# A transformer block in fp32 on one core: the second sums of weights added by a transfer from DRAM instead of by VectorE

## The chip, the core and the metric

The kernel runs on one core of a Trainium2 chip. The metric is the device time of one execution in microseconds (us), from launch to the last output byte. Engines are named as in the profile: PE is TensorE (matmuls), PEld its weight loads, DVE is VectorE, ACT is ScalarE, POOL is GpSimd, SP is SyncE. Sixteen DMA engines serve all transfers of the core. Transfers come to them from queues: q1 holds those that SP issues, q0 those that POOL issues, q10 those that ACT issues.

## What is computed

One block on 256 tokens of width 2048, all in fp32: a half-step SwiGLU feed-forward layer (2048 to 5632 and back), a mixing stage (one wide projection, attention over chunks, retention, gates, output projections), a second feed-forward layer like the first, and a last norm.

```python
def swiglu_ffn(x, w_gate, w_up, w_down):
    return (jax.nn.silu(x @ w_gate) * (x @ w_up)) @ w_down

x = x + 0.5 * swiglu_ffn(rmsnorm(x, norm_ffn1_g), ffn1_w_gate, ffn1_w_up, ffn1_w_down)
h = rmsnorm(x, norm_mix_g)
proj = h @ w_in            # q, k, v of attention; q, k, v, g of retention; two gates
...
merged = sigmoid(gate_a) * (att @ w_out_att) + sigmoid(gate_r) * (ret @ w_out_ret)
x = x + merged @ w_out
x = x + 0.5 * swiglu_ffn(rmsnorm(x, norm_ffn2_g), ffn2_w_gate, ffn2_w_up, ffn2_w_down)
return rmsnorm(x, norm_final_g)
```

## The kernel before

**Precision.** PE multiplies in a shorter format, so every weight tile is split into a high part and the rest (`split`, L138 to L142): ACT casts the tile to its high part (L140), DVE subtracts that from the tile to get the low part (L141), and each product takes three matmuls (L151, L152, L154). A tile of weights is 128 x 2 x 512 floats, 512 KB.

**Two kinds of steps.** The program is a list of steps (entries), about 1,080 in all. A standard step (`standard`) loads one tile into a ring of five raw buffers, splits it and multiplies it for both halves of the tokens, 12 matmuls. The other steps belong to groups of a Strassen-Winograd scheme (`Strassen`): two blocks of 512 output columns over the whole depth of 2048 are computed with seven products instead of eight. There are 26 groups: ten in each feed-forward layer and six in the mixing stage. A group takes 28 steps of 6 matmuls, in four phases, each over four pieces `jc` of the depth. Standard steps are woven between them (`weave`).

**The weights of a group.** For each `jc`, a group loads the upper half's tile of the first matrix (`k`) and of the second (`x`), on POOL's queue, into eight to ten kept buffers that are shared with the next group (`loads`, L540). In a feed-forward layer the first matrix is w_up and the second w_gate; in the mixing stage both are parts of w_in. Then sums are made in place:

- the first sum, x = x + k: by DVE (L529), or for one or two of the four pieces by a transfer with an add, from SBUF to SBUF (`add_on`, L545);
- the second sum, x = x + the lower tile of the second matrix: by DVE (L597), when that tile, loaded by SP into a raw buffer, is split for its own product in phase 1;
- the third, in `third`: k = x - k by DVE (L583), and x = x + the lower tile of the first matrix by a transfer with an add, straight from DRAM (L584).

A group's step is split as `r` (of a tile as it was loaded) or `s` (of a sum). In the profile a tile `hiz22610s` is the high part in group z226, phase 1, piece 0, of a sum. In phase 0 the `s` steps split the first sum, in phase 1 the second, in phase 2 k, in phase 3 the third.

**What sets the order.** Each engine works off its own list in program order and waits on semaphores. `run` goes through the steps: at step c it first prepares (splits) steps up to c + 4, then calls whatever was set for step c by `later(n, fn)`, which means n steps after the step at hand, then issues the products of step c. `load_some` issues a load as soon as a buffer of its ring is free. POOL's list therefore holds, in one order, the loads of k and x, the transfers with an add, and a few small operations; a transfer that waits holds up all behind it.

Of the kernel before, what the change touches and what calls it, by code (L numbers as in the profile page):

```python
# [11 lines left out]
ALU = mybir.AluOpType  # L12
# [33 lines left out]
FIRST_ADDED = (2, 3)  # L46
MIX_AHEAD = 12
FIRST_WAIT = 4
LAST_SUM = 24
ROTATED = {("q", 0): (6, 7), ("k", 0): (5, 6), ("q", 1): (4, 5), ("k", 1): (3, 4)}  # L50
HEAD_AT = (3, 6, 10, 13, 17, 20, 24, 27)
# [4 lines left out]
ADD_WAIT = 6  # L56
# [30 lines left out]
def block_kernel(ctx: ExitStack, tc: tile.TileContext, x, g1, w1g, w1u, w1d, gm, w_in, rel, woa, wor, wo,  # L87
                 g2, w2g, w2u, w2d, gf, cos, sin, decay, ident, out):
    nc = tc.nc
# [30 lines left out]
    def later(n, fn):  # L120
        due.setdefault(state["step"] + n, []).append(fn)

    def weights_tile(name):
        return wpool.tile([P, KC, NB], F32, tag="raw", bufs=RAW_BUFS, name=name)

    def chunk(w, r0, c0):
        return w[r0 : r0 + KC * P, c0 : c0 + NB].rearrange("(k p) n -> p k n", p=P)

    def fetch(t, w, r0, c0, parts=(slice(0, KC),)):
        for p in parts:  # L130
            nc.sync.dma_start(t[:, p, :], chunk(w, r0, c0)[:, p, :])

    def split_tiles(name):
        return [
            wpool.tile([P, KC, NB], F32R, tag=tag, bufs=SPLIT_BUFS, name=f"{tag}{name}") for tag in ("hi", "lo")
        ]

    def split(raw, name):  # L138
        hi, lo = split_tiles(name)
        nc.scalar.copy(hi, raw)  # L140
        nc.vector.tensor_sub(lo, raw, hi.bitcast(F32))  # L141
        return hi, lo  # L142
# [3 lines left out]
    def three(products, read_between=False):  # L146


        more = {"skip_group_check": True} if read_between else {}
        for acc, (ahi, alo), (whi, _), first, _ in products:  # L150
            nc.tensor.matmul(acc, ahi, whi, start=first, stop=False, **more)  # L151
            nc.tensor.matmul(acc, alo, whi, start=False, stop=False, **more)  # L152
        for acc, (ahi, _), (_, wlo), _, last in products:
            nc.tensor.matmul(acc, ahi, wlo, start=False, stop=last, **more)  # L154
# [216 lines left out]
    class Operand:  # L371


        def __init__(self, name, n):
            self.hi, self.lo, self.name = [None] * n, [None] * n, name
# [18 lines left out]
    class Norm:  # L394
# [40 lines left out]
        def put(self, b, halves=(0, 1), between=None):  # L435
# [28 lines left out]
            elif 1 in halves and b % 2 == 1:  # L464
                for i, key in enumerate(self.SUMS):
                    wait = LAST_SUM if key == "s7" and self.name != "n1" and b == D // NB - 1 else 1 + 3 * i
                    later(wait, lambda key=key: self.add_up(b // 2, key))
# [39 lines left out]
    class Strassen:  # L507
# [3 lines left out]

        def __init__(self, norm, w1, col1, w2, col2, evict, added=()):
            self.added, self.summed = added, set()
            self.add_wait, self.early = ADD_WAIT, False
            self.norm, self.w, self.col, self.evict = norm, (w1, w2), (col1, col2), evict
            self.x, self.kept, self.acc, self.wide = {}, {}, {}, {}
            self.name = f"z{len(steps)}"
# [17 lines left out]
        def loads(self):  # L535
# [11 lines left out]
            def second(jc):  # L547
# [3 lines left out]
                elif self.early:  # L551
                    later(FIRST_WAIT, lambda: self.first_once(jc))

# [16 lines left out]
        def step(self, phase, jc, of_sum):  # L570
            made = {}
            name = f"{self.name}{phase}{jc}{'rs'[of_sum]}"
            n = HALF_K // KC

            def load():
                made["raw"] = weights_tile(f"raw{name}")
                i = 2 - phase
                fetch(made["raw"], self.w[i], self.rows(1, jc), self.col[i])

            def third():  # L580

                x, k = self.x[jc], self.kept[jc]
                nc.vector.tensor_sub(k, x, k)  # L583
                nc.gpsimd.dma_start(x, chunk(self.w[0], self.rows(1, jc), self.col[0]), accum_op=ALU.add)  # L584

            def prep():
                x = self.x[jc]
                if not of_sum:
                    if phase == 0:
                        made["w"] = split(self.kept[jc], name)  # L590
                        if jc not in self.added and not self.early:
                            self.first_once(jc)
                        return
                    raw = made.pop("raw")
                    made["w"] = split(raw, name)
                    if phase == 1:
                        nc.vector.tensor_add(x, x, raw)  # L597
                elif phase == 2:
                    made["w"] = split(self.kept.pop(jc), name)
                elif phase == 3:  # L600
                    made["w"] = split(self.x.pop(jc), name)
                else:
                    if phase == 0:
                        self.first_once(jc)
                    made["w"] = split(x, name)
                    if phase == 1:
                        third()

            bank, form, fresh, closing = {
# [4 lines left out]
            }[phase, of_sum]  # L614

            def products():
                hi, lo = made["w"]
                if fresh and jc == 0:
                    self.bank(bank)
                three([  # L620
                    (
                        self.acc[bank], self.norm.form(form, KC * jc + i), (hi[:, i, :], lo[:, i, :]),
                        fresh and jc == 0 and i == 0, closing and jc == n - 1 and i == KC - 1,
                    )
                    for i in range(KC)
                ], True)
                if jc == n - 1:
                    self.end(phase, of_sum)

            loaded = not of_sum and phase in (1, 2)  # L630
            frees = ["raw"] if loaded else ["kept"] if of_sum and phase > 1 else []
            return Step(self, 0, load if loaded else None, prep, frees, products)

        def end(self, phase, of_sum):
# [563 lines left out]
    def at(step, fn):  # L1198
        due.setdefault(step, []).append(fn)
# [60 lines left out]
    for step, fn in merges:  # L1260
        at(step - 8, fn)
# [64 lines left out]
```

## Time and profile before

| | us |
|---|---|
| time, median of 3 runs | 2037.09 (2036.96 to 2037.99) |
| the profiled execution's own time | 2037.64 |
| its span, first to last instruction | 2035.9 |
| PE busy in it | 2023.9 (99%) |
| DVE busy | 1786.5 (88%) |
| ACT busy | 1504.3 (74%) |
| POOL busy | 342.9 (17%) |
| moved by DMA | 504.77 MB, mean 248 GB/s |

Busy is the time in which an engine had an instruction at work. The DMA share of a stretch is the mean over the 16 engines of the time that their packets took, divided by the stretch; packets overlap a little, so it can be over 1. A group in a feed-forward layer takes 60.73 us with the standard steps between its own, one in the mixing stage 59.80 us: such windows are used below.

### The profile page before, as it was taken

The numbers are of one execution on the slowest core, as the hardware profiler recorded it, in microseconds if no ns is written. First come the engines' busy times: TensorE is split into PE (matmuls) and PEld (weight loads), VectorE is DVE, ScalarE is ACT, GpSimd is POOL, SyncE is SP. The second block draws the span as 40 slices with busy tenths as digits, with TensorE's granted clock in tenths as the row PEclk, the third lists the DMA queues.
The fourth block names the chain that finished last, engine by engine and source line by source line (L and its number), as shares of the span: only waits on it lengthen the run. The fifth ranks groups of instructions, "written<-read, shape, count | busy, mean of one in ns | idle before, by whom it ended". The sixth has DMA issues, their size and how long they took to land.

```text
span 2035.9 us, 26220 instructions
## 1 busy us (share of the span) xinstructions
PE 2023.9 (99%) x9170; PEld 1678.8 (82%) x9170; DVE 1786.5 (88%) x1823; ACT 1504.3 (74%) x1886; POOL 342.9 (17%) x399
## 2 busy tenths in 40 slices
PE   9999999999999999999999999999999999999998
PEld 7788888888888888888888888888888888888886
DVE  7999999999998898999987677569999999999996
ACT  7788888878888777777765434557788888888885
POOL 1221122212112021111120000011112221122200
PEclk9999999999999999999999999999999999999999
DMA  9888899988878689899897645576889988889974
GB/s 311 255 249 258 255 269 281 262 240 250 260 235 237 218 232 303 273 283 286 256 320 236 209 156 185 186 247 188 263 268 276 274 243 237 258 269 270 285 199 135
DMA packets 226436, 504.77 MB, mean 248 GB/s; under 512 B 15776, under 2 KB 16480, under 8 KB 226304
## 3 DMA queue, kind: packets, MB, share of 16 engines
q1 hardware_dynamic: 154560, 297.31, 43.1%
q0 software_dynamic: 67536, 196.80, 37.4%
q10 hardware_dynamic: 4208, 8.99, 1.2%
q8 instruction: 72, 1.18, 0.2%
q14 instruction: 60, 0.49, 0.1%
HBM read 471.04 MB, written 10.50 MB: 237 GB/s over the span
## 4 chain that ended last, share of the span: by engine, by line
PE 98%; DVE 0%; DMA 0%; ACT 0%; issue 0%; POOL 0%; DVEq 0%; POOLq 0%; ACTq 0%; SPq 0%
PE acc L152 15%; PE acc L151 15%; PE acc L154 15%; DMA raw<-in_ffn_w_gate_dram 0%; PE z298a L152 0%; PE z530a L151 0%; PE z425a L151 0%; PE z850a L152 0%; PE z154a L152 0%; PE z1030a L152 0%; PE z994a L152 0%; PE z565a L151 0%; PE z742a L152 0%; PE z334a L152 0%; PE z118a L152 0%; PE z886a L152 0%
## 5 line engine op out<-in xcount | busy, mean ns | idle before, releaser
L141 DVE TENSOR_TENSOR lo<-raw,hi 128x1024 fp32r<-128x1024 f32 x351 | 427.7, 1221 | 118.7 <-ACT hi L140 113.8
L140 ACT CAST hi<-raw 128x1024 fp32r<-128x1024 f32 x351 | 368.0, 1050 | 178.0 <-PE acc L152 134.0
L808 ACT ACTIVATE xall<-acc 128x512 f32<-128x512 f32 x160 | 94.6, 591 | 13.4 <-PE acc L154 9.3
L805 ACT ACTIVATE acc<-xall 128x512 f32<-128x512 f32 x160 | 95.9, 600 | 2.5
L151 PE MATMUL acc<-hi,mgh 128*128 128x512 f32 x128 | 50.2, 392 | 0.0
L152 PE MATMUL acc<-hi,mgl 128*128 128x512 f32 x128 | 49.8, 389 | 0.0
L154 PE MATMUL acc<-lo,mgh 128*128 128x512 f32 x128 | 35.5, 390 | 0.0
L151 PE MATMUL acc<-hi,nma01h 128*128 128x512 f32 x80 | 32.0, 400 | 0.0
L151 PE MATMUL acc<-hi,nma00h 128*128 128x512 f32 x80 | 31.9, 398 | 0.0
L152 PE MATMUL acc<-hi,nma01l 128*128 128x512 f32 x80 | 31.2, 390 | 0.0
L152 PE MATMUL acc<-hi,nma00l 128*128 128x512 f32 x80 | 31.2, 390 | 0.0
L151 PE MATMUL acc<-hi,nma11h 128*128 128x512 f32 x80 | 31.2, 390 | 0.0
L151 PE MATMUL acc<-hi,nma10h 128*128 128x512 f32 x80 | 31.2, 390 | 0.0
L152 PE MATMUL acc<-hi,nma11l 128*128 128x512 f32 x80 | 31.2, 390 | 0.0
L152 PE MATMUL acc<-hi,nma10l 128*128 128x512 f32 x80 | 31.2, 390 | 0.0
L154 PEld LDWEIGHTS acc<-lo,mgh 128*128 128x128 f32 x128 | 24.0, 188 | 5.0
L151 PEld LDWEIGHTS acc<-hi,mgh 128*128 128x128 f32 x128 | 24.0, 188 | 4.9
L152 PEld LDWEIGHTS acc<-hi,mgl 128*128 128x128 f32 x128 | 24.1, 188 | 4.8
L151 PE MATMUL acc<-hi,atth 128*128 128x512 f32 x64 | 25.7, 402 | 0.0
L151 PE MATMUL acc<-hi,reth 128*128 128x512 f32 x64 | 25.3, 395 | 0.0
L359 POOL TENSOR_TENSOR n2rstd<-v,mhalf 128x2 f32<-128x2 f32 x1 | 0.7, 695 | 144.6 <-DVE v L358 144.6
L152 PE MATMUL acc<-hi,attl 128*128 128x512 f32 x64 | 25.0, 390 | 0.0
(6885 smaller groups left out, 7279.9 us busy)
## 6 DMA issues: line engine op xcount, KB each, us to landing
raw<-in_ffn_w_down_dram SPq DMA_DIRECT2D x176, 512.0 KB, 7.1
raw<-in_w_in_dram SPq DMA_DIRECT2D x80, 512.0 KB, 5.7
raw<-in_w_out_dram SPq DMA_DIRECT2D x32, 512.0 KB, 3.7
raw<-in_ffn_w_up_dram SPq DMA_DIRECT2D x16, 512.0 KB, 4.9
raw<-in_w_out_att_dram SPq DMA_DIRECT2D x16, 512.0 KB, 3.9
raw<-in_w_out_ret_dram SPq DMA_DIRECT2D x16, 512.0 KB, 3.7
raw<-in_ffn_w_gate_dram SPq DMA_DIRECT2D x15, 512.0 KB, 4.9
z390x<-in_w_in_dram POOLq DMA_DIRECT2D x8, 512.0 KB, 8.8
```

The source lines that it names most:

```text
L140: nc.scalar.copy(hi, raw)
L141: nc.vector.tensor_sub(lo, raw, hi.bitcast(F32))
L151: nc.tensor.matmul(acc, ahi, whi, start=first, stop=False, **more)
L152: nc.tensor.matmul(acc, alo, whi, start=False, stop=False, **more)
L154: nc.tensor.matmul(acc, ahi, wlo, start=False, stop=last, **more)
L359: nc.gpsimd.tensor_tensor(dst, v, mhalf[:, :width], op=ALU.pow)
L805: nc.scalar.activation(acc, xs[t][:, cols], AF.Copy, scale=2.0)
L808: nc.scalar.activation(xs[t][:, cols], acc, AF.Copy, scale=0.5)
```

## The change

In all groups, the second sum is no longer made by DVE from the raw buffer. Two entries after the one at which the first sum of a piece is split in phase 0, `second` is called: a transfer on POOL's queue that reads the lower tile of the second matrix from DRAM and adds it to x. SP's load of the same tile into a raw buffer stays, since its own product needs it; so the tile is read from DRAM twice. L597 of before is not reached any more.

```diff
+SECOND_WAIT = 2
...
         def __init__(self, norm, w1, col1, w2, col2, evict, added=()):
             self.added, self.summed = added, set()
-            self.add_wait, self.early = ADD_WAIT, False
+            self.add_wait, self.early, self.adds_second = ADD_WAIT, False, True
...
+            def second():
+                nc.gpsimd.dma_start(self.x[jc], chunk(self.w[1], self.rows(1, jc), self.col[1]), accum_op=ALU.add)
+
...
                     raw = made.pop("raw")
                     made["w"] = split(raw, name)
-                    if phase == 1:
+                    if phase == 1 and not self.adds_second:
                         nc.vector.tensor_add(x, x, raw)
...
                     if phase == 0:
                         self.first_once(jc)
                     made["w"] = split(x, name)
+                    if phase == 0 and self.adds_second:
+                        later(SECOND_WAIT, second)
                     if phase == 1:
                         third()
```

DVE's list has 1,800 rows before and 1,696 after: 104 fewer, four for each of the 26 groups. POOL's has 104 more. PE's and ACT's lists keep their order; line numbers after L48 move by one, after L580 by four or more.

POOL's list at the turn from group z226 to z262, in the first feed-forward layer, before (a name such as z226x2 is x of piece 2 of group z226; the number after the underscore is its buffer):

```order
L540 DMA z226x3_3603<-in_ffn1_w_gate_dram 128x2x512
L545 DMA z226x1_3530<-z226k1_3499 128x1024
L540 DMA z262k0_3619<-in_ffn1_w_up_dram 128x2x512
L540 DMA z262x0_3643<-in_ffn1_w_gate_dram 128x2x512
L545 DMA z262x0_3643<-z262k0_3619 128x1024
L584 DMA z226x0_3115<-in_ffn1_w_up_dram 128x2x512
L584 DMA z226x1_3530<-in_ffn1_w_up_dram 128x2x512
L584 DMA z226x2_3567<-in_ffn1_w_up_dram 128x2x512
L584 DMA z226x3_3603<-in_ffn1_w_up_dram 128x2x512
L540 DMA z262k1_4027<-in_ffn1_w_up_dram 128x2x512
```

The same place after:

```order
L541 DMA z262x0_3643<-in_ffn1_w_gate_dram 128x2x512
L546 DMA z262x0_3643<-z262k0_3619 128x1024
L582 DMA z226x0_3115<-in_ffn1_w_gate_dram 128x2x512
L582 DMA z226x1_3530<-in_ffn1_w_gate_dram 128x2x512
L582 DMA z226x2_3567<-in_ffn1_w_gate_dram 128x2x512
L582 DMA z226x3_3603<-in_ffn1_w_gate_dram 128x2x512
L588 DMA z226x0_3115<-in_ffn1_w_up_dram 128x2x512
L588 DMA z226x1_3530<-in_ffn1_w_up_dram 128x2x512
L588 DMA z226x2_3567<-in_ffn1_w_up_dram 128x2x512
L588 DMA z226x3_3603<-in_ffn1_w_up_dram 128x2x512
L541 DMA z262k1_4027<-in_ffn1_w_up_dram 128x2x512
```

Four transfers (L582) have come between the add of z262's first sum and z226's third sums; nothing else changed places.

DVE's list at phase 1 of z226, before (lo is the low part of a split; raw239 is a tile of a standard step):

```order
L141 TENSOR_TENSOR loz22610r_3812<-rawz22610r_3542,hiz22610r_3811 128x1024
L597 TENSOR_TENSOR z226x0_3115<-z226x0_3115,rawz22610r_3542 128x1024
L141 TENSOR_TENSOR loz22611r_3825<-rawz22611r_3579,hiz22611r_3824 128x1024
L597 TENSOR_TENSOR z226x1_3530<-z226x1_3530,rawz22611r_3579 128x1024
L141 TENSOR_TENSOR lo239_3840<-raw239_3677,hi239_3839 128x1024
L141 TENSOR_TENSOR loz22610s_3858<-z226x0_3115,hiz22610s_3857 128x1024
L583 TENSOR_TENSOR z226k0_3091<-z226x0_3115,z226k0_3091 128x1024
```

And after:

```order
L142 TENSOR_TENSOR loz22610r_3815<-rawz22610r_3542,hiz22610r_3814 128x1024
L142 TENSOR_TENSOR loz22611r_3828<-rawz22611r_3579,hiz22611r_3827 128x1024
L142 TENSOR_TENSOR lo239_3842<-raw239_3677,hi239_3841 128x1024
L142 TENSOR_TENSOR loz22610s_3860<-z226x0_3115,hiz22610s_3859 128x1024
L587 TENSOR_TENSOR z226k0_3091<-z226x0_3115,z226k0_3091 128x1024
```

The two adds are gone; the splits and the subtraction follow each other in the old order.

## The prediction

> **What bounds the kernel now.** First the page's busy times and slices, then what PE waited for, then the windows of single groups.
>
> ```profile
> PE 2023.9 (99%) x9170; PEld 1678.8 (82%) x9170; DVE 1786.5 (88%) x1823; ACT 1504.3 (74%) x1886; POOL 342.9 (17%) x399
> PE acc L151 <- ACT n1a00h L432: 0.6, 1, 0.6
> PE z10b L154 <- DVE loz1023r L141: 0.5, 1, 0.5
> ACT hi L140 <- PE acc L152: 134.0, 87, 3.9
> q1 hardware_dynamic: 154560, 297.31, 43.1%
> q0 software_dynamic: 67536, 196.80, 37.4%
> ```
>
> PE is busy 2023.9 of 2035.9 us, and the largest waits that the trace finds for it are of half a microsecond. ACT's longest wait in total is for PE, 134.0 us: the splits run ahead until no split buffer is free. So PE's own work sets the time, with DVE (88%) and the DMA engines (43.1 + 37.4% for the two large queues) close behind. What is taken off DVE can return at most what PE waits for DVE; what is put on the DMA engines costs nothing until they are full. So the question is how full they are in a group's period.
>
> ```profile
> 109.37:170.11 60.74, 60.74 (x275) 50.39 (x273) 56.20 (x52) 49.36 (x61) 14.05 (x16) 1.00 0.91 265
> 230.84:291.57 60.73, 60.73 (x274) 50.38 (x273) 56.62 (x53) 49.12 (x61) 12.55 (x14) 1.00 0.89 260
> 534.50:595.24 60.74, 60.74 (x275) 50.39 (x273) 56.62 (x53) 49.38 (x61) 11.03 (x12) 1.00 0.85 245
> 1448.21:1508.94 60.73, 60.73 (x274) 50.37 (x273) 56.21 (x52) 49.35 (x61) 12.54 (x14) 1.00 0.89 260
> 1630.41:1691.14 60.73, 60.73 (x274) 50.37 (x273) 56.60 (x53) 49.34 (x61) 12.51 (x14) 1.00 0.90 260
> 767.41:827.21 59.80, 59.80 (x278) 49.80 (x277) 54.02 (x49) 45.94 (x54) 11.57 (x13) 1.00 0.99 317
> 827.21:887.01 59.80, 59.80 (x266) 49.52 (x265) 56.97 (x51) 44.07 (x48) 11.59 (x13) 1.00 0.91 284
> 887.01:946.81 59.80, 59.80 (x266) 49.52 (x265) 56.85 (x52) 44.10 (x48) 11.60 (x13) 1.00 0.92 283
> 946.81:1006.61 59.80, 59.80 (x266) 49.51 (x265) 56.47 (x51) 42.00 (x46) 10.12 (x11) 1.00 0.86 256
> 1006.61:1066.41 59.80, 59.80 (x266) 49.56 (x265) 51.01 (x48) 42.05 (x46) 10.36 (x14) 1.00 0.91 288
> ```
>
> The columns after the window are its length, then PE, PEld, DVE, ACT and POOL busy with their counts, the clock, the DMA share and GB/s. The rows of 60.73 us are group periods of the feed-forward layers, of 8 in the first (its first, third and last) and 9 in the second: DVE about 56.6 us, DMA share 0.85 to 0.91, which I take as 0.89. The five of 59.80 us are the periods of the mixing stage; their mean share is 0.92.
>
> **The change part by part.**
>
> *Removed from DVE.* 104 adds.
>
> ```profile
> L597 DVE TENSOR_TENSOR z154x<-z154x,rawz15410r x1: 1218/1218/1218, 302.4 to 302.4; 128x1024 f32<-128x1024 f32 x1
> ```
>
> 104 x 1.22 = 127 us of DVE's time, 4.9 us in each period. PE waits for DVE in no period, so this is worth nothing on the path; at most the few waits above, 1 to 3 us. It does give the splits 4.9 us more room per period. I take 0.
>
> *Added to the DMA engines.* 104 transfers of 512 KB (0.524 MB) with an add, four per period. The trace has the like: the third sum of z226 is the same transfer from another matrix. The first three windows of one microsecond are those in which the first of its four pieces moved, the fourth is from its second piece; then two in which only plain loads moved, and a longer one with both kinds:
>
> ```profile
> 433.00:434.00 1.00, 1.00 (x6) 0.81 (x5) 1.00 (x2) 1.00 (x2) 0.00 (x0) 1.00 0.84 74
> 434.00:435.00 1.00, 1.00 (x6) 0.84 (x5) 1.00 (x2) 1.00 (x2) 0.00 (x0) 1.00 0.93 156
> 435.00:436.00 1.00, 1.00 (x7) 0.81 (x6) 1.00 (x2) 0.08 (x1) 0.00 (x0) 1.00 1.14 201
> 441.00:442.00 1.00, 1.00 (x6) 0.84 (x5) 1.00 (x1) 0.97 (x3) 0.00 (x0) 1.00 1.13 209
> 438.00:439.00 1.00, 1.00 (x6) 0.82 (x5) 1.00 (x2) 0.19 (x1) 0.16 (x1) 1.00 1.03 397
> 875.05:887.01 11.96, 11.96 (x54) 9.90 (x54) 10.48 (x10) 9.59 (x12) 0.00 (x0) 1.00 1.04 394
> 851.13:872.06 20.93, 20.93 (x94) 17.35 (x93) 20.23 (x20) 15.13 (x17) 8.72 (x10) 1.00 1.08 303
> ```
>
> Engines that are full move 394 GB/s of plain loads (1.33 us for a tile), but at best 209 GB/s with the add: 0.524 / 0.209 = 2.5 us, at a share of 1.13 that is 2.8 us of share. From 433.0 the share of the first third sum is 0.84 + 0.93 + 1.14 and about half of the next microsecond, some 3.4. A check from the whole period: 24 plain tiles (8 of k and x, 8 raw ones of the group, 8 of standard steps) x 1.33 x 1.04 = 33.2 of the 0.89 x 60.73 = 54.0 us; the rest, 20.8, falls on 6 transfers with an add (four third sums, two first sums), 3.5 each. So the price lies between 2.8 and 3.5 us of share; I take 3.1, nearer to the bare rate, since full engines hide a transfer's slow start.
>
> The Trainium skill ("Collectives: The Full Stack", the bandwidth ceiling) says that a reducing transfer reaches half the rate of a copy, since it reads two sources; 394 against 209 here agrees. The Trainium skill's page "DMA: Bandwidth & Descriptors" (anatomy of one DMA) counts only bytes over 436 GB/s beside a fixed delay; by an estimate from that page an added transfer takes 1.2 us and four of them 4.8 us.
>
> *What room there is.* Stretches without a pause show shares of 1.04 (plain) and 1.08 (mixed), the last two rows above; I take 1.05 as full. A feed-forward period needs 54.0 + 4 x 3.1 = 66.4 of share, and 66.4 / 1.05 = 63.3 us against 60.73: 2.5 us too much. A mixing period needs 0.92 x 59.80 + 12.4 = 67.4, or 64.2 us: 4.4 us too much. So the engines become the bound by a little in every period, and PE waits for weights.
>
> *How many periods.* 17 in the feed-forward layers and 5 in mixing. The last group of a layer, and the first one of mixing, do not count:
>
> ```profile
> 1934.08:1998.89 64.81, 64.81 (x292) 53.75 (x291) 57.05 (x53) 52.89 (x67) 4.86 (x4) 1.00 0.70 202
> 707.00:767.41 60.41, 60.41 (x272) 50.14 (x271) 59.73 (x60) 44.50 (x50) 13.18 (x15) 1.00 0.77 221
> ```
>
> At 0.70 and 0.77 four transfers fit. So 17 x 2.5 + 5 x 4.4 = 64.5 us.
>
> *What the lead absorbs.* In each of the three stages PE feels nothing until the lead of the loads is used up.
>
> ```profile
> rawz22611r<-in_ffn_w_gate_dram SPq DMA_DIRECT2D x1, 512.0 KB, 16.9
> 422.58 1.05 ACT L140 CAST hiz22611r<-rawz22611r 128x1024 fp32r<-128x1024 f32 x1
> 410.51 1.06 ACT L140 CAST hiz22601s<-z226x 128x1024 fp32r<-128x1024 f32 x1 [2.27 <-DMA z226x<-z226k]
> 395.93 0.37 SPq L131 DMA_DIRECT2D rawz22611r<-in_ffn_w_gate_dram  x1
> ```
>
> The raw tile, issued at 395.93, lands at 412.8, 9.8 us before it is split; but ACT already waits 2.27 us for the first sum that POOL adds. Between 2 and 10 us, then; 5 us as an estimate, 15 us for three stages. 64.5 - 15 leaves **about 50 us**.
>
> *The waits that are added.* A second sum waits for the splits of the first sum; behind it on POOL stand the other second sums, then the third sums, then the next group's loads, all of which need later work anyway. ACT's cast of phase 1's first sum now waits for the second sum, and behind it on ACT stand the casts and evictions on which PE depends.
>
> ```profile
> 414.80 0.95 POOL L545 DMA_DIRECT2D z262x<-z262k  x1 [12.72 <-DMA z262x<-in_ffn_w_gate_dram]
> DMA to landing us min/median/max: 5.0/5.0/5.0
> 431.29 1.22 POOL L584 DMA_DIRECT2D z226x<-in_ffn_w_up_dram  x1 [15.54 <-ACT xall L808]
> 425.75 1.06 ACT L140 CAST hiz22610s<-z226x 128x1024 fp32r<-128x1024 f32 x1 [0.59 <-PE acc L152]
> 432.14 1.04 ACT L140 CAST hiz22611s<-z226x 128x1024 fp32r<-128x1024 f32 x1
> 413.50:416.00 2.50, 2.50 (x14) 2.13 (x13) 2.50 (x3) 2.19 (x4) 0.95 (x1) 1.00 0.06 23
> ```
>
> POOL is free from 415.8 to 431.3, so z226's second sums go out right behind the add at 414.80, which lands 5.0 us later, at 419.8. In the first period the first of them lands near 423 and the second near 426 to 428, wanted at 425.75 and 432.14. So the waits alone cost nothing while the queues are empty at that place (share 0.06 from 413.5); they cost as soon as the loads of the stretch before end some 3 us later, which the overfull period brings about. I price them at 0 beside the sum. On SP, the raw buffer of phase 1 is free one add (1.1 us) earlier; that only makes loads wait in the queue.
>
> *The sum.* 2037.64 (profiled execution) + 50 = 2087.6, and with the 0.55 us by which the median of the runs lies lower, **2087 us**, 2.5% more.
>
> *Both ends.* Low: 2.5 us for each transfer in engines that are full at 1.08. A feed-forward period has (1 - 0.89/1.08) x 60.73 = 10.7 us free for 10.0, nothing lost; a mixing period 8.9 us, 1.1 lost, which the lead takes. That gives 2037. High: 3.5 us, and pauses stay as they are, so that full is 1.00: 54.0 + 14.0 = 68.0, 7.3 too much in 17 periods, and 69.0, 9.2 too much in 5: 170 us, 2207.
>
> **The rivals.**
>
> *There is room after all (same).* The mechanism: second sums run in the gap that the engines have at the turn from phase 0 to phase 1 of each group, and the bare price of 2.5 us holds. The gap is there (share 0.06 at 413.5), and the mixed stretch with its share of 1.08 shows that the two kinds can interleave without a pause. It decides at the point where four transfers take no more than the 9.3 us that a period has free at a full share of 1.05 (1 - 0.89/1.05, x 60.73), 2.3 us each. Against it: no window shows more than 209 GB/s with the add, and mixing has less room. Time: 2037. By the estimate of 4.8 us from the Trainium skill's page on DMA it would come out so.
>
> *The gaps cannot be filled (much slower).* Transfers are issued only when a buffer or a sum is ready, so the pauses stay and the added 3.1 to 3.5 us lie end to end: the high end, 2150 to 2207. For it: a late second sum delays the third sum, and that the next group's loads. Against it: the gap lies just where the second sums go.
>
> *DVE was pacing PE (faster).* DVE has 56.6 of 60.73 us busy. If PE's three waits went, and nothing else came, 2034 to 2036. That is under what can be measured; only stalls that the trace hides could make it more.
>
> **How the numbers follow.** The full engines as summed (2040 to 2145): 0.64. Much slower: 0.12. Room after all: 0.20. Faster: 0.04. A measurement of this kernel can tell about 0.2% (4 us) from no change. So slower 0.76, same 0.20, faster 0.04. The range from 2036 to 2145 leaves out the much slower case and the faster one, 0.16 together.
>
> **What would show it.** In the changed kernel's windows of a feed-forward period the DMA share should stand at 1.0 or more nearly throughout, the period should be 62 to 64 us instead of 60.73, and that of mixing 63 to 65 of 59.80. PE's list of waits should name L141 or L140, and ACT's should name DMA into x or raw, with some microseconds in each period from the second or third group of a stage on. q0 should hold 251 MB, DVE's busy time should be 1660 us. If the period stays at 60.73 with a share near 1.0, the price of a transfer was too high; if the share stays at 0.9 and PE waits all the same, it is the chain of waits and not the engines' work. If DVE's relief shows in PE, the first step was wrong.

## The result, and the profile after

The changed kernel takes 2069.44 us (median; 2067.19 to 2072.1), against 2037.39 for the kernel before on the same chip: a ratio of 1.0157, 95% interval 1.0145 to 1.017. It is 32 us slower; 50 were forecast, with a range of 2036 to 2145. The profiled execution took 2072.1 us, 34.5 more than that of before, and the stages below are read from these two.

The page of the changed kernel, with the lines that answer to those of before: busy times, DMA queues (packets, MB, share of 16 engines), the chain that ended last by engine, and the bytes read.

```profile
PE 2042.6 (99%) x9170; PEld 1673.1 (81%) x9170; DVE 1679.9 (81%) x1719; ACT 1490.2 (72%) x1886; POOL 469.8 (23%) x503
q0 software_dynamic: 95824, 251.33, 50.3%
q1 hardware_dynamic: 154560, 297.31, 41.3%
PE 76%; DMA 12%; ACT 4%; DVE 3%; issue 2%; DVEq 0%; ACTq 0%; POOLq 0%; POOL 0%
HBM read 525.57 MB, written 10.50 MB: 259 GB/s over the span
```

DVE lost 106.6 us of busy time for 104 instructions, less than 104 x 1.22, since instructions in a row overlap at their ends (in the trace of before one starts 1.14 us after the other). POOL's queue q0 carries 54.5 MB more. The chain that ended last was 98% PE before; now PE holds 76% of it and DMA 12%. PE's own busy time rose by 18.7 us with the same 9,170 matmuls: half of the loss hides inside matmuls whose ends are modelled, so a list of PE's waits shows only the rest.

Before, the same chain, and ACT's waits for raw loads (who waited for whom, us in total, times, longest):

```profile
PE 98%; DVE 0%; DMA 0%; ACT 0%; issue 0%; POOL 0%; DVEq 0%; POOLq 0%; ACTq 0%; SPq 0%
ACT hi L140 <- DMA raw<-in_ffn_w_down_dram: 2.9, 3, 1.8
ACT hi L140 <- DMA raw<-in_w_in_dram: 7.5, 7, 2.5
```

Then the waits of the changed kernel:

```profile
PE acc L152 <- ACT hi L141: 10.1, 15, 1.4
ACT hi L141 <- DMA raw<-in_ffn_w_down_dram: 86.5, 41, 3.8
ACT hi L141 <- DMA raw<-in_w_in_dram: 25.1, 13, 2.9
```

Before, ACT waited for loads of w_down 2.9 us in all, and for raw loads of w_in 7.5. Now it is 86.5 and 25.1, and PE waits for that ACT. None of these tiles is a second sum. They are raw tiles of standard steps, which SP loads over q1. Its waits for the groups' own raw tiles (rawz in the profile) come on top, some 34 us in 27 waits; for second sums it waited four times, some 5 us in all.

Last, the windows of group periods in the changed kernel (length, engines' busy times, clock, DMA share, GB/s), the fourth being the last group of the first layer, where the loads thin out:

```profile
234.68:298.05 63.37, 61.85 (x274) 50.06 (x273) 53.01 (x49) 49.26 (x62) 17.43 (x18) 1.00 1.03 291
422.99:484.84 61.85, 61.55 (x274) 50.14 (x273) 52.61 (x49) 48.54 (x61) 17.41 (x18) 1.00 1.02 287
1471.16:1531.89 60.73, 60.73 (x274) 50.37 (x273) 51.96 (x48) 48.66 (x61) 17.41 (x18) 1.00 1.03 287
609.47:674.72 65.25, 65.25 (x294) 53.82 (x292) 53.59 (x52) 53.08 (x67) 15.14 (x17) 1.00 0.85 232
```

A period of 60.73 us has become 61.75 to 63.37 (the first of the second layer is still 60.73), at a DMA share of 1.01 to 1.03 where it was 0.89. In the last group of a layer (share 0.85) nothing is lost: 65.25 us, 65.24 before. By stage, read at PE's transposes (the last of the mixing norm, the last of retention, that of the second layer's last group): up to the mixing norm 14.2 us are lost, from there to retention 9.1 (526.81 us instead of 517.76), from there to the end 11.4.

The periods of the mixing stage, read from the first matmul of one group to that of the next, are not all of 59.80 us: the first is (z425), the other four take 57.12. Here are the first, second and last of before, then the same of the changed kernel:

```profile
766.35:826.14 59.79, 59.79 (x277) 49.80 (x276) 54.01 (x49) 45.68 (x52) 11.57 (x13) 1.00 0.99 317
826.14:883.26 57.12, 57.12 (x253) 47.31 (x252) 54.29 (x49) 41.84 (x46) 11.59 (x13) 1.00 0.91 279
997.50:1054.62 57.12, 57.12 (x253) 47.31 (x252) 52.65 (x48) 42.03 (x47) 9.59 (x12) 1.00 0.83 254
780.58:845.75 65.17, 62.58 (x278) 49.01 (x276) 49.53 (x44) 45.23 (x53) 16.52 (x17) 1.00 1.07 324
845.75:903.55 57.80, 57.52 (x254) 47.22 (x252) 50.76 (x46) 41.00 (x47) 16.41 (x17) 1.00 1.03 295
1020.79:1077.91 57.12, 57.12 (x253) 47.30 (x252) 49.12 (x44) 42.26 (x47) 14.39 (x16) 1.00 1.04 302
```

The first period, fullest before (0.99), loses 5.4 us; the three after it 0.7, 1.9 and 1.1; the last, at 0.83 before, nothing.

*Inside one period.* POOL's and SP's lists in the changed kernel at z226 (start, length, what), then how long the two loads of w_down that were issued at 431.5 and 435.1 took to land, the casts that wait for them, and two windows of one microsecond (packets, MB and share of each queue): one with work in both queues, one with plain loads alone.

```profile
425.06 0.92 POOL L546 DMA_DIRECT2D z262x<-z262k  x1 [12.62 <-DMA z262x<-in_ffn_w_gate_dram]
425.65 2.80 POOL L582 DMA_DIRECT2D z226x<-in_ffn_w_gate_dram  x2
429.54 2.42 POOL L582 DMA_DIRECT2D z226x<-in_ffn_w_gate_dram  x2 [1.09 <-DVE loz22602s L142]
431.53 0.37 SPq L132 DMA_DIRECT2D raw<-in_ffn_w_down_dram  x1
435.06 1.71 SPq L132 DMA_DIRECT2D raw<-in_ffn_w_down_dram  x2
raw<-in_ffn_w_down_dram SPq DMA_DIRECT2D x1, 512.0 KB, 9.2
raw<-in_ffn_w_down_dram SPq DMA_DIRECT2D x1, 512.0 KB, 13.7
440.83 1.05 ACT L141 CAST hi<-raw 128x1024 fp32r<-128x1024 f32 x1 [2.72 <-DMA raw<-in_ffn_w_down_dram]
448.84 1.05 ACT L141 CAST hi<-raw 128x1024 fp32r<-128x1024 f32 x1 [2.89 <-DMA raw<-in_ffn_w_down_dram]
...
q0 software_dynamic: 62, 0.13, 70.6%
q1 hardware_dynamic: 63, 0.12, 36.3%
...
q1 hardware_dynamic: 216, 0.41, 105.9%
```

While both queues have work they move the same number of packets, 62 and 63 in a microsecond. A packet with an add takes twice the time (70.6% for 62, 36.3% for 63), and a raw load gets 0.12 MB/us where it has 0.41 alone: 4.4 us for a tile instead of 1.3, with another tile or two ahead of it. (The same rate beside plain copies is shown with the second experiment.) In this state from 430 to 449, a load issued when one of the five raw buffers came free lands 9 to 14 us later, and its cast waits 2.7 and 2.9 us.

The Trainium skill ("DMA: Bandwidth & Descriptors", queues, rings and completion order) says that each DMA engine takes turns between the queues that have work, a packet at a time; 62 packets against 63 agree. Its figure of bytes over 436 GB/s (anatomy of one DMA), 1.2 us for a tile by an estimate from that page, is near what the plain copies of the second experiment below take (1.20 to 1.34 us), and not what the add takes (2.48 to 2.61 us).

### The profile page after: what moved, and what is told of

It reads as the page before. It is cut to its first block, busy times and chain, and to the rows that moved or that the text cites. A ratio compares the mean times of both kernels' runs of the same rounds, so it can differ in the third digit from the quotient of the medians.

```text
span 2070.3 us, 26320 instructions
## 1 busy us (share of the span) xinstructions
PE 2042.6 (99%) x9170; PEld 1673.1 (81%) x9170; DVE 1679.9 (81%) x1719; ACT 1490.2 (72%) x1886; POOL 469.8 (23%) x503
## 3 DMA queue, kind: packets, MB, share of 16 engines
q0 software_dynamic: 95824, 251.33, 50.3%
q1 hardware_dynamic: 154560, 297.31, 41.3%
## 4 chain that ended last, share of the span: by engine, by line
PE 76%; DMA 12%; ACT 4%; DVE 3%; issue 2%; DVEq 0%; ACTq 0%; POOLq 0%; POOL 0%
PE acc L155 12%; PE acc L152 11%; PE acc L153 11%; DMA raw<-in_ffn_w_down_dram 10%; ACT hi L141 2%; DMA raw<-in_w_in_dram 1%; DVE lo L142 1%; DMA rawz42522r<-in_w_in_dram 1%; ACT xall L814 1%; ACT acc L811 0%; PE z1030a L152 0%; PE z334a L153 0%; PE z886a L153 0%; PE z742a L155 0%; PE z886a L152 0%
## 5 line engine op out<-in xcount | busy, mean ns | idle before, releaser
L155 PE MATMUL acc<-lo,nma01h 128*128 128x512 f32 x80 | 24.9, 392 | 0.4 <-DVE lo L142 0.3
```

## Experiments

Each ratio is to the kernel before on the same chip, with its 95% interval. "Sum of work" is the theory of the prediction: the DMA engines have more to do in a period than they can. "Slow turn" is the one that the profile after suggests: the work fits, but raw loads crawl beside the second sums and their lead is too short.

**The two halves of the change alone.** First only what it removes: the kernel before without its second sums.

```diff
-                    if phase == 1:
-                        nc.vector.tensor_add(x, x, raw)
```

> The kernel before, with the second sums left out (phase 1's sum, phase 2's k and phase 3's sum lack the lower tile of the second matrix). It measures DVE's relief alone: 104 adds of 1.22 us off DVE, no transfer added. Theory 'the DMA engines have too much work' and theory 'raw loads get only every other turn beside the second sums' both say 2037 us, within 2 us of the kernel before; the DMA share of a feed-forward period stays at 0.89. If DVE had paced PE it would be 2030 or less.

Measured 2035.60 us, 0.9991 (0.9982 to 1.0001). DVE's relief is worth 1.8 us in the medians, though the interval takes in no change. In the trace 1.7 us arise before the first group ends: that group's transposes stand at 107.67 us instead of 109.37, and every feed-forward period after is 60.73 us as before. So DVE did not pace PE in the periods.

Then what it adds, without the add in the transfer:

```diff
-                nc.gpsimd.dma_start(self.x[jc], chunk(self.w[1], self.rows(1, jc), self.col[1]), accum_op=ALU.add)
+                nc.gpsimd.dma_start(self.x[jc], chunk(self.w[1], self.rows(1, jc), self.col[1]))
```

> The changed kernel with the four transfers per group as plain copies over x (the upper tiles' sum is overwritten, so the sums of phases 1 to 3 lack it). Same bytes, same places and waits, no add in the transfer. If the price is that of the add (half rate), four plain tiles take 4 x 1.33 = 5.3 us of the 9.3 us that a feed-forward period has free, and the time is 2037 to 2042 us. If it is the bytes, or that POOL's list and ACT's casts wait for one more transfer, it stays above 2055.

Measured 2035.65 us, 0.9992 (0.9983 to 1.0001), the same as with nothing added. The DMA queues of this kernel:

```profile
q0 software_dynamic: 82512, 251.33, 43.6%
q1 hardware_dynamic: 154560, 297.31, 43.1%
```

The bytes are those of the changed kernel, 251.33 MB. The two queues' packets took 86.7% of 2034.5 us, 1763.9 us of the 16 engines, where the kernel before took 80.5% of 2035.9 us, 1638.9: 1.20 us for each of 104 transfers. In the changed kernel it is 91.6% of 2070.3 us, 1896.4, or 2.48 us each. Counted from the run without second sums (35.6 + 44.3% of 2033.6 us, 1624.8) the two are 1.34 and 2.61 us: packet times of the same traffic differ that much between two kernels. So 54.5 MB more from DRAM, 104 more transfers on POOL's list and ACT's wait for them cost nothing; **the add in the transfer is the price**, by about doubling the engines' time.

The raw loads get no more beside plain copies than beside adds. First a microsecond of this kernel in which second transfers move beside raw loads, then 12 us of the kernel before with plain loads in both queues; last, the median time for a raw tile of w_down to land, before, here and in the changed kernel:

```profile
q0 software_dynamic: 66, 0.26, 66.7%
q1 hardware_dynamic: 72, 0.12, 32.6%
...
q0 software_dynamic: 765, 2.81, 60.4%
q1 hardware_dynamic: 767, 1.48, 33.7%
...
raw<-in_ffn_w_down_dram SPq DMA_DIRECT2D x176, 512.0 KB, 7.1
raw<-in_ffn_w_down_dram SPq DMA_DIRECT2D x176, 512.0 KB, 8.3
raw<-in_ffn_w_down_dram SPq DMA_DIRECT2D x176, 512.0 KB, 10.9
```

It is one packet for one there too, and 0.12 MB/us for the raw loads: the plain packets of q0 carry some 4 KB and take 0.16 us (66.7% of 16 engines for 66), nearly as long as those of 2 KB with an add (0.18). But a tile is 144 such packets by q0's counts (82,512 less 67,536, for 104 tiles), and 272 with an add (95,824 less 67,536). By these counts the add does not make the raw loads crawl more; it makes them crawl for about twice as long.

**The dose, and the place.** Half of the second sums by transfer, the other half by DVE:

```diff
-                    if phase == 1 and not self.adds_second:
+                    if phase == 1 and not (self.adds_second and jc in SECOND_ADDED):
...
-                    if phase == 0 and self.adds_second:
+                    if phase == 0 and self.adds_second and jc in SECOND_ADDED:
```

with pieces 2 and 3 in SECOND_ADDED,

> The changed kernel with the second sums of pieces 2 and 3 by transfer and those of 0 and 1 by DVE from the raw buffer, as before. Theory 'too much work': two transfers take about 5 us of the 9.3 us free in a feed-forward period, 4.8 of about 7.4 in mixing, so 2037 to 2040 us. Theory 'every other turn': the stretch of slow raw loads is half as long, and a quarter to a half of the loss stays: 2042 to 2053 us.

or pieces 0 and 1:

> The changed kernel with the second sums of pieces 0 and 1 by transfer, 2 and 3 by DVE. Theory 'sum of work': as with pieces 2 and 3, 2037 us. Theory 'slow turn': two in a row, 2037 to 2045; pieces 0 and 1 are wanted first, behind the shortest lead (10 and 7 us from issue to cast where 2 and 3 have 15 to 20), so if the second sums' own lateness counted it would show here and not with 2 and 3.

Measured 2037.01 us, 0.9998 (0.9989 to 1.0008), and 2035.65 us, 0.9993 (0.9984 to 1.0003). That is where the theory 'sum of work' put it, not 'slow turn' (2042 to 2053 with pieces 2 and 3). Two per period cost nothing that the medians show, whichever they are; so the second sums' own lateness is not the cost either. Only the trace with pieces 2 and 3 has a loss: its first period in mixing is 1.8 us longer than before. The period with pieces 2 and 3:

```profile
230.22:290.95 60.73, 60.73 (x274) 50.38 (x273) 54.83 (x51) 49.38 (x61) 14.90 (x16) 1.00 0.97 277
```

Eight transfers with an add in a feed-forward period, share 0.97, nothing lost. The other way to eight: all four second sums by transfer, but the first sums by DVE.

```diff
-ADDED = (0, 1)
+ADDED = ()
-MIX_ADDED = (0,)
+MIX_ADDED = ()
-FIRST_ADDED = (2, 3)
+FIRST_ADDED = ()
```

> The changed kernel with all first sums made by DVE (no transfer from SBUF to SBUF with an add): eight transfers with an add per feed-forward period instead of ten, eight per mixing period instead of nine. That is the number of the run with half of the second sums by transfer, 2037.0 us, but here the four second sums still stand in a row. Theory 'sum of work': the place does not matter, 2037 to 2042 us (some mixing loss stays, with one transfer less only). Theory 'slow turn of the raw loads beside four second sums in a row': most of the loss stays, 2052 to 2069 us.

Measured 2053.44 us, 1.0079 (1.0064 to 1.0094): half of the loss stayed, as the slow turn foretold. But its waits name another cause than that theory's, so the same edit was made to the kernel before:

> Control: the kernel before with all first sums made by DVE (second sums by DVE too). It has six transfers with an add less per pair of groups and no DMA shortage. If the 0.87 us per feed-forward period that the run with all first sums by DVE lost is the chain DVE add, ACT cast, DVE subtraction at piece 0, this loses as much or more: 2050 to 2075 us. If that loss was of the DMA engines: 2037 us.

Measured 2053.67 us, 1.0079 (1.0061 to 1.0097): the same. The longest entry of PE's waits with all first sums by DVE, after the change and without it:

```profile
PE acc L155 <- DVE lo L142: 8.8, 16, 0.6
PE acc L154 <- DVE lo L141: 9.3, 17, 0.6
```

At each group's start DVE's adds stand between the splits (the chain goes from the add, L530, through DVE's subtractions to PE), and a period of a feed-forward layer takes 61.6 us, 0.87 more, with or without the second sums by transfer. So with eight transfers in a period the second sums cost nothing on top of that here either (the longer period leaves the loads some more time), and the mixing stage shows it by itself: 517.76 us from one transpose to the other, as before the change, against 526.81 in the changed kernel. This run, read by its time alone, would have been put down to the slow turn, though DVE's chain made it.

One transfer of first sums left in the feed-forward layers (piece 0) and none in mixing avoids that chain at piece 0:

```diff
-ADDED = (0, 1)
+ADDED = (0,)
-MIX_ADDED = (0,)
+MIX_ADDED = ()
```

> The changed kernel with the first sum of piece 1 made by DVE instead of by transfer in the feed-forward layers (piece 0 stays a transfer), and all first sums by DVE in the mixing stage: nine transfers with an add per feed-forward period, eight per mixing period. If the DMA engines' load decides: mixing loses nothing (as with all first sums by DVE), the feed-forward periods lose between 0 and half of what they do with ten: 2036 to 2048 us. If DVE's first sums cost by themselves, whichever piece: 2050 us or more.

Measured 2043.86 us, 1.0035 (1.0021 to 1.0048). Mixing with eight again loses nothing (517.76 us). The feed-forward layers with nine lose 4.1 and 1.8 us, where ten cost 14.2 and 11.4; how much of that is the DVE's first sum of piece 1 was not separated.

**Lead or sum.** Six raw buffers instead of five, for one activation buffer less:

```diff
-RAW_BUFS = 5
+RAW_BUFS = 6
-ACT_TILES = 30
+ACT_TILES = 29
```

> The changed kernel with six raw buffers instead of five (and 29 instead of 30 activation buffers). Theory 'too much work': the engines are full anyway, a longer lead is used up once per stage, at most 5 us come back: 2064 to 2069 us. Theory 'raw loads get only every other turn for some 20 us in each period': a load that starts a step earlier lands before it is wanted, and at least half of the 32 us come back: 2037 to 2053 us.

> Control: the kernel before with six raw buffers and 29 activation buffers. All theories: 2037 us within 2 us, since PE waited for no load.

Measured 2053.09 us, 1.0076 (1.0061 to 1.0091), and the control 2037.74 us, 1.0002 (0.9993 to 1.0011). Half of the loss is gone with the same work. Seven (and 28):

> The changed kernel with seven raw buffers (and 28 activation buffers). Six brought back 16 of 32 us: periods of 60.73 us now stand beside some of 62.5 to 63. Theory 'the work just fits, the lead of the raw loads is too short for the slow turn': one buffer more brings back most of the rest, 2037 to 2045 us. Theory 'the work's sum is over the engines' rate, and a longer lead is used up once': no more than 3 us come back, 2048 to 2055 us.

Measured 2041.94 us, 1.0024 (1.0015 to 1.0034). (Seven buffers in the kernel before were not run.) Two of its periods:

```profile
289.88:350.61 60.73, 60.73 (x274) 50.39 (x273) 52.71 (x49) 49.55 (x61) 17.41 (x18) 1.00 1.05 294
350.61:411.35 60.74, 60.74 (x275) 50.41 (x273) 52.55 (x49) 49.33 (x61) 17.42 (x18) 1.00 1.05 295
```

Ten transfers with an add in 60.73 us, at a share of 1.05, the level that I had taken for full, and PE loses nothing: so it is in all periods of both feed-forward layers, which are back (1.7 us faster and 0.3 us faster than before). So in these layers the work's sum fits, and the loss was one of lead. Only mixing still loses, 5.9 us, most of it in one wait:

```profile
PE z495a L152 <- ACT z495c L662: 4.1, 1, 4.1
ACT z495c L662 <- DMA raw<-in_w_in_dram: 5.1, 1, 5.1
```

**Starting earlier.** The second sums stand on POOL's list behind the next group's first-sum transfer, which waits 12.6 us for a load. At the end of that wait, and until the second sums move, the engines' share is down (it is over 1 in the 10 us ahead of it):

```profile
422.99:425.49 2.50, 2.50 (x16) 2.21 (x15) 2.50 (x3) 2.29 (x4) 0.43 (x1) 1.00 0.43 159
425.49:427.99 2.50, 2.50 (x12) 2.07 (x12) 2.50 (x4) 1.49 (x2) 2.50 (x3) 1.00 0.69 129
```

So that transfer was moved behind them:

```diff
-                    later(self.add_wait, lambda: add_on(jc))
+                    later(self.add_wait + (8 if jc == 0 else 0), lambda: add_on(jc))
```

> The changed kernel with the next group's first-sum transfer of piece 0 moved on POOL's list behind the four second sums (it has 50 us until its use), so that the second sums can start some 5 to 6 us earlier, in the pause in which the DMA engines stand at a share of 0.4 to 0.9. Same work. If the work's sum in engines that never pause were the limit: 2064 to 2070 us. If the pause and the late start of the second sums are: 4 to 5 us per period are there to be filled, 2040 to 2055 us.

Measured 2092.58 us, 1.0273 (1.0254 to 1.0293): slower than either theory said. A period of it, and two waits:

```profile
303.64:366.50 62.86, 61.56 (x275) 50.15 (x273) 52.37 (x49) 49.15 (x61) 17.45 (x18) 1.00 1.02 284
ACT hiz42500s L141 <- DMA z425x<-z425k: 11.1, 1, 11.1
ACT hiz4600s L141 <- DMA z46x<-z46k: 8.2, 1, 8.2
```

The periods within a layer stay at some 62.3 us on average (498.1 us for the eight of the first layer, 499.2 in the changed kernel), so the earlier start brought nothing. Most of the further loss comes where a layer begins: there piece 0 of the second group is loaded late, its first sum is wanted soon, and the 50 us that I had counted on for it do not exist. In mixing about half of it lies in the later periods; why was not traced.

**Both remedies together.** Seven raw buffers, and no first sum by transfer in mixing:

```diff
-RAW_BUFS = 5
+RAW_BUFS = 7
-ACT_TILES = 30
+ACT_TILES = 28
-MIX_ADDED = (0,)
+MIX_ADDED = ()
```

> The changed kernel with seven raw buffers, and the first sums of the mixing stage all by DVE. All 104 second sums are made by transfer. If the two causes left are the lead of the raw loads in the feed-forward layers (seven buffers lost nothing there) and the ninth transfer with an add per period in mixing (eight lost nothing there), nothing of the loss stays and DVE's relief at the start shows: 2035 to 2038 us, like the run with the second sums left out. If the two share a third cause, 4 us or more stay: 2041 us.

Measured 2035.51 us, 0.9992 (0.9983 to 1.0001). All 104 second sums are transfers with an add, and the time is that of the kernel in which they are left out (2035.60). The loss is accounted for in full. With the run of pieces 0 and 1 by transfer (2035.65) it is the fastest version here that computes the whole block, 1.8 us below the kernel before, which is not clear of what a measurement can tell.

## Why the prediction was right, and where not

The direction and the cause in the large were right: DVE's relief does not reach PE, the added transfers load the DMA engines up to their limit, and PE ends up waiting for weights. The steps:

- *DVE's adds are worth nothing on the path, at most 1 to 3 us*: 1.8 us, nearly all of it at the first group. (PE's longest wait was 1.3 us, for POOL, in the kernel's first 7 us, and not half a microsecond; the sum does not use it.)
- *Price of a transfer*, "I take 3.1", between 2.8 and 3.5 us: **mis-sized**. Both queues together take 2.48 us more for each, or 2.61 counted from the run without second sums; the bare time of 2.5 us, which the prediction also had, came nearest. Its reason, that full engines hide a transfer's slow start, is not shown: q0 alone took 2.69 us more for each (37.4% of 2035.9 us, then 50.3% of 2070.3), and the rest is that q1's same 154,560 packets took 22 us less (43.1%, then 41.3%). Why they did stays open.
- *Full is a share of 1.05*: near enough. Seven raw buffers hold that level over whole periods with nothing lost; the first period of mixing reaches 1.07.
- *A feed-forward period needs 66.4 of share, 2.5 us too much*: it is 63.8 (1.05 x 60.73 in the run with seven buffers, 2.44 for each transfer beside the 54.0), and that just fits. This is **the step that failed in kind**: the periods did not grow because the work overran the engines, but because the raw loads lost their turn at a lead of five buffers. That gave 1.0 to 2.6 us per period, by another road than the 2.5 of the sum; that the sizes are alike is luck.
- *Mixing, 4.4 us in each of five periods*: 9.1 us in all, and not evenly: 5.4 in the period whose share was 0.99 before, none in that of 0.83. The prediction took one mean share, 0.92, and windows of 59.80 us for all five, where four periods have 57.12. Here the work is close to the limit even with seven buffers (5.9 us left), and one transfer less per period ends it.
- *The lead absorbs 5 us per stage*: hardly. The second layer's first period lost nothing; in the first layer the very first one lost 1.0 us already.
- *The added waits cost nothing by themselves*: right for POOL's and ACT's wait for the second sums (the plain copies have the same waits and cost nothing). What was missed is SP's queue, which the text only said would wait: the raw loads, above all those of standard steps, which the change does not touch, were the ones that came late.

Of the rivals, "room after all" came closest in the sum: its deciding point, 2.3 us of engine time each, is 2.44 / 1.05, what the runs show. It took no account of who waits while the engines are just full. Most signs named beforehand came as told: share 1.02, feed-forward periods near 62 us, ACT's waits naming DMA into raw, q0 at 251 MB. Not so mixing's periods (57.1 to 65.2 us, where 63 to 65 were named) and DVE's busy time (1679.9 us, not 1660).

## What to carry over

When work moves from an engine to the DMA queues, count a transfer with an add as about two plain ones (2.48 to 2.61 us of the engines against 1.20 to 1.34 here), and look beyond the share: the first to suffer are the transfers on the other queue that have the shortest lead, even if the change does not touch them. Here a raw load fell to the same 0.12 MB/us beside plain copies as beside adds, and lost PE's time only where that lasted too long for its lead; it must then start earlier, by more buffers, or the adds must be fewer. And where an experiment lands on a theory's number, read which wait made it, and make the same edit to the kernel before.

## What the runs showed that was not expected

Plain loads of one queue beside the transfers of another do not keep their share of bytes but one packet for one: 0.12 MB/us against 0.41 alone, beside adds and beside plain copies alike. And an add in flight costs about the engine time of a second transfer: 2.48 us against 1.20 for 512 KB, over 104 of them (2.61 against 1.34 by the other count).
